# Layer 1's value projections as one of 512 columns with a new order around the first head pairs, and layer 0's stick-breaking weights by sigmoids

## The chip, the core and the metric

The kernel runs as one program on one core of a Trainium2 chip. The core has a matrix engine (TensorE, PE in the profile; its weight loads are PEld), three engines for elementwise work (VectorE or DVE, ScalarE or ACT, GpSimd or POOL), a queue engine that issues most transfers (SyncE, SP), a scratch memory (SBUF) and eight accumulator banks of 128 x 512 fp32 (PSUM) that TensorE writes and the others read. Each engine works through its own list of instructions in order; semaphores between the lists make one engine wait for another. The metric is the device time of one execution in microseconds (us), as the median of several runs.

## The reference, cut to what matters

A decoder trunk with two layers: 256 tokens, width 1024, 16 heads of 64, everything in fp32. Layer 0 mixes by stick-breaking attention, layer 1 by a sparse attention whose keys and values come from one projection of the stream after layer 0; each layer ends with an MLP of 4096 hidden columns and a squared ReLU.

```python
# layer 0, stick-breaking: causal is key < query
z = einsum('bqhd,bshd->bhqs', q, k) * 64 ** -0.5
log_1m = where(causal, log_sigmoid(-z), 0)
excl = cumsum(log_1m, axis=3, reverse=True) - log_1m
a = where(causal, exp(log_sigmoid(z) + excl), 0)
o = einsum('bhqs,bshd->bqhd', a, v)
```

So the weight of a key is sigmoid(z) of that key times the product of sigmoid(-z) over the keys between it and the query.

```python
# layer 1: three branches with gates, keys and values shared by 4 heads
kv = (rms_norm(h) @ w_kv)            # 3 branches x (k, v) x 4 groups x 64
hid = gelu(blk @ cmp_w1); k_cmp, v_cmp = hid @ cmp_w2   # 15 overlapping blocks of 32 tokens
p_cmp = softmax(q . k_cmp / 8)       # compressed branch
p_sel = softmax(rope(q) . k_sel / 8) # selected blocks: 16 of 4, so all of them, causal
p_win = softmax(rope(q) . k_win / 8) # window of 512 tokens, so all of them, causal
out = sum over branches of gate * (p @ v)
```

With 256 tokens both the selected and the window branch are plain causal attention, each with its own keys and values: in each head there are two score matrices, two softmaxes and two products with values, beside the small compressed branch.

## The kernel before, in words

**Precision.** A product of fp32 quality is made of fp32r matmuls: each operand is split into a high part (a cast) and a low part (operand less high part), and `mm3` issues three products, high by high, high by low and low by high. Weights arrive by DMA as `raw` (128x1024), ScalarE casts them to `wh` (L372), VectorE subtracts to get `wl` (L387). All matmuls are issued in L487, all transposes through TensorE in L499.

**What sets the order.** TensorE's list is written out by hand, call by call, in `layer0`, `mlp` and `layer1`. The other engines' lists are made by a planner, `Order`, which runs while the kernel is built: it keeps a clock that each matmul moves on by its estimated cost, and queues of ready steps. A chain (`go(gen, rank)`) is a series of steps, each with an estimated cost and with the engines that may do it: A is ScalarE, D VectorE, G GpSimd. Whenever an engine is free by the planner's clock, it is given the ready step of the lowest rank. `o.need(chain)` ahead of matmuls moves the clock on to the chain's end. The result is a fixed list for each engine; on the chip the engines then run these lists with semaphores, whatever the estimates were.

**Banks.** `B(i, name)` takes PSUM bank i. Matmuls that begin a new tile in a bank wait until the tile that was there has been read out. In layer 1's attention four banks, `Z = (4,5,6,3)`, hold the scores of one head pair; bank 7 holds the accumulator of the q projection (`qp`), banks 1, 2, 0 and sometimes 7 serve the rest.

**Layer 0's attention.** Eight head pairs, two a group. `proj` makes q and k transposed (58 to 64 matmuls between two groups' scores); q is scaled by 0.125 times the token's inverse norm, k by the inverse norm (`rbq`). `scores` writes each head's scores, 384 columns (keys of both blocks for the later queries, of one for the earlier), into a bank. `soft` works on a pair: VectorE takes the minimum with a table (`cap`, 40 where allowed, -1e30 where not) out of PSUM into `sbe`, ScalarE takes exp and ln(1 + x), VectorE runs a scan of sums from the last key to the first that stops at marks (`go_on`), subtracts, and ScalarE takes exp once more (L957 to L965). `turn` transposes the weights, `values` multiplies them with v.

**Layer 1's attention.** `kv_proj` twice (512 columns each: compressed keys and values, then the keys of the other two branches), with the gather of the compressed blocks (`gather_tr`) inside the second; `q_proj` for four groups of four heads, each 48 matmuls of 256 columns in bank 7; `cw_proj` for the compressed blocks' hidden layer. Then eight head pairs, each with

- `scores(p)`: two matmuls of 512 and two of 256 columns into `Z`;
- per pair eight mask passes on VectorE (L1359: add the causal table, minimum as side result), eight exponentials on ScalarE with the sums (L1361), then reciprocal, product with the gates and three scalings of `pe` by L1388 (GpSimd) or L1389 (VectorE);
- `turn(p, 0..2, bank)`: four transposes each into a bank (`ptp`), which ScalarE or VectorE copies to `pT` (L1414).

The value projection is done in two parts, `v_proj(br, 1, ...)`, one a branch, 256 columns for each of the two token blocks, both in bank 1; VectorE or ScalarE evicts each block with its inverse norm (L1119, `vs`). Between these stand the steps of the compressed branch: `cmp_turn` (transposes of the hidden layer, copied to `hidT`, L1466), `cmp_keys`, `cmp_scores` (`psc`), `cmp_soft` (transposes to `psct`, then six small VectorE steps, L1528 to L1537, and two exponentials), `cmp_probs`. `values(g)` multiplies with `vs` and makes the split output `oT` (L576, L577), `part` is a piece of the output projection (`acc`).

The order of the calls in layer 1, cut to the part in question:

```python
v_proj(1, 1, 0, 4); cmp_soft(0, ...)
turn(2, 0, 2); turn(2, 1, 7); v_proj(1, 1, 4, NK)
turn(2, 2, 2); scores(4, Z)
q_proj(3, 7, 0, 4); cmp_probs(0, ...); turn(3, 0, 2); turn(3, 1, 1)
q_proj(3, 7, 4, NK); turn(3, 2, 2)
oc[0] = values(0, 0); cmp_scores(1, 7); scores(5, Z); turn(4, 0, 2)
part(0, 0); ...
```

Of the kernel before, what the change touches and what calls it, by code (L numbers as in the profile page):

```python
# [17 lines left out]
T = 2  # L18
# [10 lines left out]
R_GELU, R_SCT, R_SOFT = 0.7, 0.85, 0.9  # L29
# [5 lines left out]
C_CAP, C_ANY, C_COS, C_SIN, C_BLK, C_PW, C_ROT, C_ROS, C_CMT, C_CB, C_END = (  # L35
    0, 384, 386, 418, 450, 458, 462, 718, 974, 1230, 1486)

SEG = P + 1
ROW = 3 * SEG
# [134 lines left out]
def hybrid_kernel(ctx, tc, x, xt, eye, gcols, gfin, wqk, wv, wo0, wkv, wvs, wq, wg, wo1, w1, w2, cw1, cw2, cpos, gate_b, consts, out):  # L174
# [13 lines left out]
    nc.scalar.preload_act_table_set("natural_log_exp_and_others")  # L188
# [74 lines left out]
    i_kv = [[feed2(wkv[n, i]) for i in range(2)] for n in range(2)]  # L263
    i_c = [[[], []], [[], []]]
    i_vs, i_q = [], []
# [6 lines left out]
    i_q.append(feed2(wq[0]))  # L272
# [544 lines left out]
    def layer0(ap):  # L817
# [84 lines left out]
        rbq = ap.tile([P, 2, T * P], F32, name="rbq", bufs=1)  # L902
# [4 lines left out]
        def rb(i):  # L907
            if i:
                yield dve(256, lambda: nc.vector.tensor_copy(rbq[:, 1, :], pr[:, 0:T * P]))
            else:  # L910
                yield dve(256, lambda: nc.vector.tensor_scalar(rbq[:, 0, :], pr[:, 0:T * P], 0.125, None, op0=OP.mult))

        rbc = [go(rb(i)) for i in range(2)]
# [9 lines left out]
        def proj(p, s0, s1):  # L923
            for s in range(s0, s1):
# [11 lines left out]
                if s % 16 == 15:  # L936
# [3 lines left out]
                    def gen(a=a, qk=qk, q=qkT[:, a]):  # L940
                        u = ap.tile([P, T * P], F32, name="qku", bufs=2)
                        yield act(256, lambda: nc.scalar.copy(u, qk[:, T * P:]))
                        yield dve(256, lambda: nc.vector.tensor_add(q, qk[:, 0:T * P], u))
                        yield rbc[a]
                        yield {"D": (420, lambda: nc.vector.tensor_mul(q, q, rbq[:, a]), True),
                               "G": (620, lambda: nc.gpsimd.tensor_mul(q, q, rbq[:, a]), True)}
                    ch.append(go(gen(), 0.8))

        cap = cst[:, C_CAP:C_CAP + 3 * P].rearrange("p (b c) -> p b c", b=3)

        def soft(z, got):
            e = ap.tile([P, 2 * ROW], F32, name="sbe", bufs=3)
            s = ap.tile([P, 2 * ROW], F32, name="sbs", bufs=2)
            nc.gpsimd.memset(e.rearrange("p (b c) -> p b c", b=6)[:, :, P:SEG], NEG)

            def low(hd):
                return dve(384, lambda: nc.vector.tensor_tensor(  # L957
                    e[:, hd * ROW:(hd + 1) * ROW].rearrange("p (b c) -> p b c", b=3)[:, :, 0:P],
                    z[hd][:, 0:384].rearrange("p (b c) -> p b c", b=3), cap, op=OP.min))
            yield [low(0), low(1)]  # L960
            yield act(774, lambda: nc.scalar.activation(s, e, AF.Exp))
            yield act(774, lambda: nc.scalar.activation(s, s, AF.Ln, bias=1.0))
            yield dve(774, lambda: nc.vector.tensor_tensor_scan(s[:, ::-1], s[:, ::-1], go_on[:, ::-1], 0.0, OP.add, OP.mult), 810, True)
            yield {"D": (956, lambda: nc.vector.tensor_sub(e, e, s), True)}
            yield act(774, lambda: nc.scalar.activation(e, e, AF.Exp))  # L965
            got.append(e)

        def scores(g):
# [7 lines left out]
            for j in range(2):  # L976
# [7 lines left out]
                live["e", 2 * g + j] = got, go(soft(zs[j], got), 1 + 0.01 * g)  # L984
            o.tick(90)

        def turn(g, i, b):
# [5 lines left out]
            for c in range(4):  # L993
# [3 lines left out]
                p0 = hd * ROW + (2, 0, 1)[m] * SEG  # L997
# [78 lines left out]
    def layer1(xk, pt0, ch, ap):  # L1076
# [24 lines left out]
        smallc = go(small(), 3, 6000)  # L1101
# [32 lines left out]
        def value_out(br, t, pk):  # L1134
            yield scaled(vs[t][:, br, :], pk[:, t * 256:(t + 1) * 256], t, 256)
# [4 lines left out]
        def kv_proj(n, banks, mid=None):  # L1140
            pk = [B(b, "pk") for b in banks]
            for k in range(NK):
                if k == 4 and mid is not None:
                    mid()
                if n == 0 and k == 2:
# [22 lines left out]
        def v_proj(br, b, k0, k1):  # L1168
            if k0 == 0:
                pvs[br] = B(b, "pk")  # L1170
            pk = pvs[br]
            for k in range(k0, k1):
                w, c = W(i_vs[br][k // 4]), k % 4 * 256
                for t in range(T):
                    mm3(pk[:, t * 256:(t + 1) * 256], tok(xk, k, t), cut(w, c, c + 256),
                        k == 0 and t == 0, k == NK - 1)
                if k % 4 == 3:
                    gone(i_vs[br][k // 4])
            if k1 < NK:
# [687 lines left out]
```

## Time and profile before

| | |
|---|---|
| median of three runs | 596.75 us (596.1, 596.9, 596.75) |
| the profiled execution | 595.99 us, span 594.2 us |
| value projection and layer 0's attention | about 0 to 27 and 27 to 113 us of the span |
| first MLP | about 113 to 283 us |
| layer 1: projections and attention | about 283 to 418 us, PE busy 134.55 of 135 |
| second MLP and end | about 418 to 594 us |

The rows are of one profiled execution. The page gives for each engine the busy time, its share of the span and the number of instructions; PEclk is the clock that TensorE was granted, in tenths. The chain of waits follows the work that ended last back to the start. In a row of the timeline the columns are start, length, engine, line, operation, what is written and read with its size, and count; in brackets the idle time ahead and what ended it. Rows of groups give busy time, mean length in ns, and the idle time ahead of them. Rows of stretches give the length, then the busy time of PE, PEld, VectorE, ScalarE and GpSimd with counts, the granted clock, the share of the DMA engines and GB/s. The length of a TensorE row holds its drain: matmuls that follow each other overlap, and the distance of two starts is what one costs.

### The profile page before, as it was taken

The numbers are of one execution on the slowest core, as the hardware profiler recorded it, in microseconds if no ns is written. First come the engines' busy times: TensorE is split into PE (matmuls) and PEld (weight loads), VectorE is DVE, ScalarE is ACT, GpSimd is POOL, SyncE is SP. The second block draws the span as 40 slices with busy tenths as digits, with TensorE's granted clock in tenths as the row PEclk, the third lists the DMA queues.
The fourth block names the chain that finished last, engine by engine and source line by source line (L and its number), as shares of the span: only waits on it lengthen the run. The fifth ranks groups of instructions, "written<-read, shape, count | busy, mean of one in ns | idle before, by whom it ended". The sixth has DMA issues, their size and how long they took to land.

```text
span 594.2 us, 9360 instructions
## 1 busy us (share of the span) xinstructions
PE 586.0 (99%) x3346; PEld 492.2 (83%) x3346; DVE 520.0 (88%) x829; ACT 434.9 (73%) x701; POOL 98.3 (17%) x116
## 2 busy tenths in 40 slices
PE   9999999999999999999999999999999999999995
PEld 6888887888888888888888888677888888888884
DVE  6698997589999999998885899964889999999976
ACT  6767667587888978984934796572888888888963
POOL 0013330001211212000120443330001121211001
PEclk9999999999999999999999999999999999999998
DMA  8983334389977899555554634304499787997401
GB/s 317 400 298 105 124 123 148 108 316 372 261 229 235 238 261 265 151 150 185 193 169 152 249 107 156 129 1 141 138 405 322 210 256 217 294 237 225 106 1 71
DMA packets 38063, 119.83 MB, mean 202 GB/s; under 512 B 4608, under 2 KB 5888, under 8 KB 38016
## 3 DMA queue, kind: packets, MB, share of 16 engines
q1 hardware_dynamic: 31248, 107.01, 50.8%
q0 software_dynamic: 6336, 11.54, 11.8%
q10 hardware_dynamic: 432, 0.69, 0.3%
q8 instruction: 26, 0.43, 0.3%
q14 instruction: 21, 0.17, 0.1%
HBM read 118.17 MB, written 1.05 MB: 201 GB/s over the span
## 4 chain that ended last, share of the span: by engine, by line
PE 93%; ACT 4%; DMA 2%; DVE 0%; SPq 0%; issue 0%; POOLq 0%; POOL 0%; ACTq 0%
PE acc L487 34%; PE pu L487 30%; PE qk L487 8%; PE pk L487 4%; PE po L487 3%; PE qp L487 3%; PE pv L487 3%; PE z L487 2%; ACT pe L1361 2%; PE ptp L499 1%; ACT wh L372 1%; DMA rv<-in_wv 1%; PE ph L487 1%; PE pt L499 1%; PE pa L499 1%; DMA raw<-in_wq 1%
## 5 line engine op out<-in xcount | busy, mean ns | idle before, releaser
L387 DVE TENSOR_TENSOR wl<-raw,wh 128x1024 fp32r<-128x1024 f32 x132 | 163.5, 1255 | 11.1 <-ACT wh L372 10.9
L372 ACT CAST wh<-raw 128x1024 fp32r<-128x1024 f32 x132 | 135.6, 1052 | 27.7 <-DMA raw<-in_wq 8.9
L487 PE MATMUL pu<-xn,wh 128*128 128x512 f32 x512 | 128.4, 390 | 0.0
L487 PEld LDWEIGHTS pu<-xn,wh 128*128 128x128 f32 x512 | 94.8, 188 | 18.8
L487 PEld LDWEIGHTS pu<-xn,wl 128*128 128x128 f32 x512 | 70.9, 190 | 5.7
L487 PE MATMUL pu<-xn,wl 128*128 128x256 f32 x512 | 72.6, 282 | 0.0
L487 PE MATMUL acc<-wh,hh 128*128 128x512 f32 (+1 forms) x136 | 53.2, 392 | 0.0
L487 PE MATMUL acc<-wl,hh 128*128 128x512 f32 (+1 forms) x136 | 53.1, 390 | 0.0
L487 PE MATMUL acc<-wh,hl 128*128 128x512 f32 (+1 forms) x136 | 52.7, 388 | 0.0
L674 ACT COPY mu<-pu 128x512 f32<-128x512 f32 x64 | 37.4, 584 | 19.1 <-PE pu L487 18.9
L394 POOL DMA_DIRECT2D fours<-in_w x24 | 21.5, 896 | 147.5 <-DVE ms L707 69.4
L487 PE MATMUL acc<-wh,oT 128*128 128x512 f32 x128 | 43.2, 401 | 0.0
L394 POOL DMA_DIRECT2D four<-in_w x20 | 19.5, 977 | 142.2 <-DMA four<-in_w 65.0
L696 DVE TENSOR_TENSOR hl<-ms,hh 128x1024 fp32r<-128x1024 f32 (+2 forms) x36 | 36.4, 1014 | 3.3 <-ACT hh L695 2.9
L487 PE MATMUL acc<-th,hh 128*128 128x512 f32 x96 | 37.7, 393 | 0.0
L487 PE MATMUL acc<-tl,hh 128*128 128x512 f32 x96 | 37.6, 392 | 0.0
L487 PE MATMUL acc<-th,hl 128*128 128x512 f32 x96 | 37.4, 389 | 0.0
L695 ACT CAST hh<-ms 128x1024 fp32r<-128x1024 f32 (+2 forms) x36 | 31.6, 884 | 2.6 <-DVE ms L707 2.3
L487 PE MATMUL pk<-wh,xk 128*128 128x512 f32 (+1 forms) x128 | 32.9, 340 | 0.0
L1361 ACT ACTIVATE pe<-pe,nm 128x256 f32<-128x256 f32 (+1 forms) x64 | 28.5, 448 | 5.6 <-DVE nm L1359 5.6
L487 PE MATMUL qk<-xa,wh 128*128 128x512 f32 x128 | 32.5, 395 | 0.0
L1388 POOL TENSOR_TENSOR pe<-pe,rs 128x512 f32<-128x512 f32 x17 | 22.1, 1315 | 50.0 <-DVE rs L1378 42.8
(225 smaller groups left out, 1224.2 us busy)
## 6 DMA issues: line engine op xcount, KB each, us to landing
raw<-in_w SPq DMA_DIRECT2D x80, 512.0 KB, 6.2
four<-in_w SPq DMA_DIRECT2D x24, 512.0 KB, 6.9
fours<-in_w SPq DMA_DIRECT2D x24, 512.0 KB, 7.6
raw<-in_wqk SPq DMA_DIRECT2D x16, 512.0 KB, 6.1
raw<-in_wo SPq DMA_DIRECT2D x16, 512.0 KB, 4.0
fours<-in_w POOLq DMA_DIRECT2D x24, 256.0 KB, 4.9
four<-in_w POOLq DMA_DIRECT2D x20, 256.0 KB, 6.6
raw<-in_wkv SPq DMA_DIRECT2D x8, 512.0 KB, 4.5
```

Of the source, the lines that this page charges most:

```text
L372: k = {"A": (195 + 0.835 * m, lambda: nc.scalar.copy(a, b), False), "D": (200 + 0.49 * m, lambda: nc.vector.tensor_copy(a, b), True)}
L387: yield {"D": (150 + 1.045 * m, lambda: nc.vector.tensor_sub(lo, raw, f32(hi)), True)}
L394: nc.gpsimd.dma_start(to, other, accum_op=OP.add)
L487: nc.tensor.matmul(o_, a, b, start=first, stop=last, skip_group_check=True)
L499: nc.tensor.transpose(o_, a, i)
L674: yield act(512, lambda: nc.scalar.copy(u[:, f, :], pu[f]))
L695: yield act((b - a) * P, lambda: nc.scalar.copy(hh[:, into], flat[:, q]))
L696: yield dve((b - a) * P, lambda: nc.vector.tensor_sub(hl[:, into], flat[:, q], f32(hh[:, into])), port=True)
L1361: act(n, lambda: nc.scalar.activation(d, d, AF.Exp, bias=nm[:, i:i + 1], scale=-1.0, accum_out=rs[:, t, hd, b:b + 1]), 150)]
L1388: return {"G": (1040, lambda: nc.gpsimd.tensor_tensor(s, s, f, op=OP.mult), True), "D": (690, lambda: nc.vector.tensor_tensor(s, s, f, op= ...
```

## The change

**Layer 1's values.** One projection of 512 columns (both branches) takes the place of two of 256. It has an accumulator for each token block, in banks 1 and 7, and its weights are stored and fetched in blocks of 512 columns. VectorE or ScalarE evicts 512 columns at once.

**Layer 1's list of calls** is rewritten: the scores and transposes of the first pairs come earlier, the value projection stands in four pieces between pairs 1 and 4, the steps of the compressed branch stand elsewhere, and the transposes of pairs 0 to 3 use other banks. The weights are fetched in the new order of use, on the same queue. The second `kv_proj` is called in two pieces with the gather between. The planner's ranks of the copies of q's input (2.5 to 1.0) and of the small tables (3 to 1.5) change, `scores` lets the planner wait until the former pair's scores were read (`zread`), and slots of `pT` and of the gathered blocks change places.

**Layer 0's weights.** Scores are no longer scaled by q's inverse norm; a sigmoid reads them out of PSUM with the token's scale, 0.125 times the inverse norm, with a minus for the factors of the product and a plus for the key's own weight: eight sigmoids a pair, four of 256 and four of 128 columns. VectorE's scan multiplies, with a 1 added at each query's own place (`begins`, an identity written by ScalarE), so that masked keys come out as zero; one product follows. The minimum with `cap`, the exponentials and the logarithm of the weights are gone. The table of functions that ScalarE loads at the start is the one with the sigmoid; the one with exp and ln is loaded in layer 1.

```diff
@@ feeds
-    i_q.append(feed2(wq[1]))
-    feed_cw(1)
-    i_vs.append(feed2(wvs[0]))
-    i_q.append(feed2(wq[2]))
-    i_vs.append(feed2(wvs[1]))
-    i_q.append(feed2(wq[3]))
+    feed_q(1)
+    feed_cw(1)
+    feed_q(2)
+    feed_v()
+    feed_q(3)
...
@@ layer0
-            yield [low(0), low(1)]
-            yield act(774, lambda: nc.scalar.activation(s, e, AF.Exp))
-            yield act(774, lambda: nc.scalar.activation(s, s, AF.Ln, bias=1.0))
-            yield dve(774, lambda: nc.vector.tensor_tensor_scan(s[:, ::-1], s[:, ::-1], go_on[:, ::-1], 0.0, OP.add, OP.mult), 810, True)
-            yield {"D": (956, lambda: nc.vector.tensor_sub(e, e, s), True)}
-            yield act(774, lambda: nc.scalar.activation(e, e, AF.Exp))
+            def sig(to, hd, t, i):
+                src = z[hd][:, 0:256] if t else z[hd][:, 256:384]
+                dst = to[:, hd * HW:hd * HW + 256] if t else to[:, hd * HW + 257:hd * HW + 385]
+                return act(128 + 128 * t, lambda: nc.scalar.activation(dst, src, AF.Sigmoid, scale=by[:, t, i:i + 1]), 95)
+            yield begun
+            yield byc
+            yield [sig(f, hd, t, 0) for t in (1, 0) for hd in range(2)]
+            nc.gpsimd.memset(e.rearrange("p (h c) -> p h c", h=2)[:, :, 256:HW:129], 0.0)
+            yield [dve(772, lambda: nc.vector.tensor_tensor_scan(
+                f[:, ::-1], f[:, ::-1], begins[:, ::-1], 0.0, OP.mult, OP.add), 810, True)] + [
+                sig(e, hd, t, 1) for t in (1, 0) for hd in range(2)]
+            yield {"D": (956, lambda: nc.vector.tensor_mul(e[:, 0:2 * HW - 1], e[:, 0:2 * HW - 1], f[:, 1:2 * HW]), True)}
...
@@ layer1
-        def value_out(br, t, pk):
-            yield scaled(vs[t][:, br, :], pk[:, t * 256:(t + 1) * 256], t, 256)
+        def value_out(t):
+            yield scaled(vs[t].rearrange("p b c -> p (b c)"), pvs[t], t, 512)
...
+        def v_proj(k0, k1):
+            for t in range(T if k0 == 0 else 0):
+                pvs[t] = B((1, 7)[t], "pk")
             for k in range(k0, k1):
-                w, c = W(i_vs[br][k // 4]), k % 4 * 256
+                w, c = W(i_vs[k // 2]), k % 2 * 512
                 for t in range(T):
-                    mm3(pk[:, t * 256:(t + 1) * 256], tok(xk, k, t), cut(w, c, c + 256),
-                        k == 0 and t == 0, k == NK - 1)
+                    mm3(pvs[t], tok(xk, k, t), cut(w, c, c + 512), k == 0, k == NK - 1)
...
+            if k1 == NK:
+                vsc.extend(go(value_out(t), 1.1) for t in range(T))
...
+        q_proj(1, 7, 0, 2)
         scores(0, Z)
-        q_proj(1, 7)
+        q_proj(1, 7, 2, 6)
+        scores(1, Z)
+        q_proj(1, 7, 6, NK)
         cw_proj(1)
         hc = go(gelu(), R_GELU)
-        scores(1, Z)
-        v_proj(0, 1, 0, 4)
         turn(0, 0, 2)
-        turn(0, 1, 0)
-        v_proj(0, 1, 4, NK)
+        turn(0, 1, 1)
         turn(0, 2, 2)
         q_proj(2, 7, 0, 2)
-        cmp["tc"] = cmp_turn(0)
         scores(2, Z)
-        q_proj(2, 7, 2, 4)
+        q_proj(2, 7, 2, 5)
+        turn(1, 0, 2)
+        turn(1, 1, 0)
+        q_proj(2, 7, 5, NK)
+        cmp["tc"] = cmp_turn(1)
+        turn(1, 2, 2)
+        v_proj(0, 2)
         cmp["kc"] = cmp_keys(0)
-        q_proj(2, 7, 4, 5)
-        turn(1, 0, 2)
-        turn(1, 1, 1)
-        q_proj(2, 7, 5, NK)
-        turn(1, 2, 2)
+        scores(3, Z)
+        v_proj(2, 4)
         cmp["s0"] = cmp_scores(0, 0)
-        scores(3, Z)
-        v_proj(1, 1, 0, 4)
-        cmp["s0"] = cmp_soft(0, *cmp["s0"], 0)
         turn(2, 0, 2)
-        turn(2, 1, 7)
-        v_proj(1, 1, 4, NK)
+        turn(2, 1, 2)
+        v_proj(4, 6)
         turn(2, 2, 2)
         scores(4, Z)
+        cmp["s0"] = cmp_soft(0, *cmp["s0"], 0)
+        v_proj(6, NK)
         q_proj(3, 7, 0, 4)
+        turn(3, 0, 2)
+        turn(3, 1, 2)
+        q_proj(3, 7, 4, 6)
+        scores(5, Z)
         pcc[0].append(cmp_probs(0, cmp["s0"], 0))
-        turn(3, 0, 2)
-        turn(3, 1, 1)
-        q_proj(3, 7, 4, NK)
+        q_proj(3, 7, 6, NK)
         turn(3, 2, 2)
         oT = o_tiles(0)
         oc[0] = values(0, 0)
+        turn(4, 0, 2)
         cmp["s1"] = cmp_scores(1, 7)
-        scores(5, Z)
-        turn(4, 0, 2)
         part(0, 0)
```

The lists that the planner made of it, at three places. A name with a number is one buffer of that name; a bracket names the engines whose semaphores the instruction waits for.

TensorE's list before, from the end of the second value projection (`pk`) over the last transposes of pair 2 (`ptp`) and the scores of pair 4 (`z`) to the first matmuls of q of group 3 (`qp`, bank 7):

```order
L487 MATMUL pk<-wl,xk 128x256
L487 MATMUL pk<-wh,xk 128x256
L499 MATMUL ptp<-ident,pe 128x128 [waits Activation_49]
L499 MATMUL ptp<-ident,pe 128x128 x3
L487 MATMUL z_3817<-kT,qm 128x512
L487 MATMUL z_3818<-kT,qm 128x512
L487 MATMUL z_3819<-kT,qm 128x256
L487 MATMUL z_3820<-kT,qm 128x256
L487 MATMUL qp<-xq,wh 128x256 [waits Activation_49]
```

and now:

```order
L497 MATMUL psct<-cw2s,hv 120x64 x4
L509 MATMUL psct<-ident,sct 128x128 x2
L497 MATMUL pk<-wh,xk 128x512
L497 MATMUL pk<-wl,xk 128x512
L497 MATMUL pk<-wh,xk 128x512 x2
...
L497 MATMUL pk<-wh,xk 128x512
L497 MATMUL qp<-xq,wh 128x256 [waits DVE_49]
L497 MATMUL qp<-xq,wh 128x256
L497 MATMUL qp<-xq,wl 128x256
```

The scores and transposes that stood between the last value matmul and q of group 3 now stand ahead of the last 12 value matmuls; q's first matmul follows these directly and waits for VectorE.

VectorE's list now, from the copy of pair 2's second transposes to the evictions of the two value accumulators (`vs`); mask passes of pair 4 (L1383), steps of the compressed softmax (`cmx`, `ce`, `csm`), a weight split (`wl`) and a scaling of pair 3 (L1415):

```order
L1440 COPY pT<-ptp 128x512
L1404 TENSOR_TENSOR rs<-rs,gates 128x8
L397 TENSOR_TENSOR wl<-raw,wh 128x1024
L1383 ISA pe,nm<-z_3741,causal 128x256
...
L1554 TENSOR_REDUCE cmx<-psct 128x16
...
L1415 TENSOR_TENSOR pe<-pe,rs 128x512
...
L1562 TENSOR_TENSOR csm<-csm,gany 128x16
...
L1563 TENSOR_TENSOR ce<-ce,csm 128x240
L1383 ISA pe,nm<-z_3744,causal 128x128
L1383 ISA nm 128x1
L1139 TENSOR_SCALAR vs_2919<-pk,r 128x512
L1139 TENSOR_SCALAR vs_2920<-pk,r 128x512
```

Before, the evictions of 256 columns stood ahead of the mask passes of pair 4; now they stand behind all eight (four of 256 columns and four of 128) and behind the softmax.

TensorE's list at the first two transposes of pair 2, before:

```order
L487 MATMUL psct<-cw2s,hv 120x64 x3
L499 MATMUL psct<-ident,sct 128x128 x2
L499 MATMUL ptp<-ident,pe 128x128 [waits DVE_49,Activation_49]
L499 MATMUL ptp<-ident,pe 128x128 [waits Pool_49]
L499 MATMUL ptp<-ident,pe 128x128
L499 MATMUL ptp<-ident,pe 128x128 [waits Activation_49]
L499 MATMUL ptp<-ident,pe 128x128 x3
L499 MATMUL ptp<-ident,pe 128x128 [waits Pool_49]
L487 MATMUL pk<-wh,xk 128x256
```

and now (`psc` are the compressed scores):

```order
L497 MATMUL psc<-qu,kcb 32x256 [waits DVE_49,PE_49]
L497 MATMUL psc<-qu,kcb 32x256 x3
L509 MATMUL ptp<-ident,pe 128x128 [waits DVE_49,Activation_49]
L509 MATMUL ptp<-ident,pe 128x128 [waits Pool_49]
L509 MATMUL ptp<-ident,pe 128x128
L509 MATMUL ptp<-ident,pe 128x128 [waits Activation_49]
L509 MATMUL ptp<-ident,pe 128x128 [waits DVE_49]
L509 MATMUL ptp<-ident,pe 128x128 x2
L509 MATMUL ptp<-ident,pe 128x128 [waits Pool_49]
L497 MATMUL pk<-wh,xk 128x512
```

The second four transposes, which went to bank 7, now go to bank 2 as the first four do, and their first one waits for VectorE, which copies the first four.

More of the change, by code (lines that the diff above doesn't have):

```diff
@@ L33 @@
 GELU_C = 2.0 * 0.7978845608028654
[L35 to L39, printed above, removed]
+C_ANY, C_COS, C_SIN, C_BLK, C_PW, C_ROT, C_ROS, C_CMT, C_CB, C_END = (
+    0, 2, 34, 66, 74, 78, 334, 590, 846, 1102)
+HW = 3 * P + 2
 LAG = 200
@@ L262, in hybrid_kernel, with feed_kv, feed_q, feed_v @@
     i_m = [feed_mlp(0)]
-    i_kv = [[feed2(wkv[n, i]) for i in range(2)] for n in range(2)]
+    i_kv = [None, None]
     i_c = [[[], []], [[], []]]
-    i_vs, i_q = [], []
+    i_vs, i_q = [], [None] * NG
+    def feed_kv(n):
+        i_kv[n] = [feed2(wkv[n, i]) for i in range(2)]
+    def feed_q(g):
+        i_q[g] = feed2(wq[g])
+    def feed_v():
+        for i in range(2):
+            i_vs.extend(feed2(wvs[i]))
     def feed_cw(i):
@@ L893, in layer0, with starts @@
         pump()
-        go_on = ap.tile([P, 2 * ROW], BF16, name="go_on", bufs=1)
-        nc.gpsimd.memset(go_on, 1.0)
-        nc.gpsimd.memset(go_on.rearrange("p (h c) -> p h c", h=2)[:, :, 2 * SEG - 1:ROW:SEG], 0.0)
+        begins = ap.tile([P, 2 * HW], BF16, name="begins", bufs=1)
+        nc.gpsimd.memset(begins, 0.0)
+        fs = [ap.tile([P, 2 * HW], F32, name=f"sbf{i}", bufs=1) for i in range(2)]
+        for f in fs:
+            nc.gpsimd.memset(f, 0.0)
+        def starts():
+            b2 = begins.rearrange("p (h c) -> p h c", h=2)
+            for c in (P, 2 * P + 1):
+                yield act(256, lambda: nc.scalar.copy(b2[:, :, c:c + P], ident[:, None, :].to_broadcast([P, 2, P])))
+        begun = Chain(o, starts(), 1.5, ws.landed)
         v_first(0)
@@ L905, in layer0, with rb, scale @@
             mm(pr[:, t * P:(t + 1) * P], rstd[t].to_broadcast([P, P]), ident, t == 0, True, 4.0)
[L907 to L913, printed above, removed]
+        def rb():
+            yield dve(256, lambda: nc.vector.tensor_copy(rbq, pr[:, 0:T * P]))
+        def scale():
+            for t in range(T):
+                for i in range(2):
+                    yield dve(1, lambda: nc.vector.tensor_scalar(by[:, t, i:i + 1], rstd[t], (-0.125, 0.125)[i], None, op0=OP.mult))
+        rbc, byc = go(rb()), go(scale())
         def v_out(n, t):
@@ L1132, in key_out, with kv_proj @@
             yield pool(128, lambda: nc.gpsimd.tensor_add(src[:, :, 0:16], a, b), 60)
-        def value_out(br, t, pk):
-            yield scaled(vs[t][:, br, :], pk[:, t * 256:(t + 1) * 256], t, 256)
+        def value_out(t):
+            yield scaled(vs[t].rearrange("p b c -> p (b c)"), pvs[t], t, 512)
         def first_out(t, pk):
             yield scaled(kd0[:, t], pk.rearrange("p (m d) -> p m d", d=DH), t, 512)
[L1140 to L1144, printed above, removed]
+        pks = {}
+        def kv_proj(n, banks, k0, k1):
+            if k0 == 0:
+                pks[n] = [B(b, "pk") for b in banks]
+            pk = pks[n]
+            for k in range(k0, k1):
                 if n == 0 and k == 2:
@@ L1337, in scores @@
             o.need(qch[g], *kc)
+            o.need(*zread)
+            zread.clear()
             z1 = [B(banks[hd], "z1").rearrange("p (b k) -> p b k", b=2) for hd in range(2)]
@@ L1541, in cmp_probs @@
         def cmp_probs(f, c, b):
-            o.need(c)
+            o.need(c, *pcc[f])
             pt = B(b, "pct")
```

85 lines of the change are left out of this document (40 added, 45 removed).

## The prediction

> **What bounds the kernel now.** Read the page's busy times first, then the chain that ended last, then stretches of 10 us.
>
> ```profile
> span 594.2 us, 9360 instructions
> PE 586.0 (99%) x3346; PEld 492.2 (83%) x3346; DVE 520.0 (88%) x829; ACT 434.9 (73%) x701; POOL 98.3 (17%) x116
> PEclk9999999999999999999999999999999999999998
> PE 93%; ACT 4%; DMA 2%; DVE 0%; SPq 0%; issue 0%; POOLq 0%; POOL 0%; ACTq 0%
> ```
>
> TensorE is busy for 99% of the span, at a clock that is granted throughout, and 93% of the last chain is its own matmuls. So the end moves only with what TensorE issues and with the time in which it stands still. The other engines count only where they make it wait. How near that is differs by stage:
>
> ```profile
> 60.00:70.00 10.00, 10.00 (x62) 8.92 (x61) 10.00 (x11) 7.59 (x12) 4.30 (x3) 1.00 0.18 59
> 340.00:350.00 10.00, 10.00 (x81) 8.21 (x82) 9.72 (x28) 10.00 (x23) 3.18 (x3) 1.00 0.35 124
> 350.00:360.00 10.00, 9.58 (x79) 8.54 (x78) 9.92 (x33) 8.47 (x29) 6.23 (x5) 1.00 0.21 70
> 360.00:370.00 10.00, 10.00 (x86) 8.74 (x86) 9.79 (x30) 7.84 (x23) 3.01 (x4) 1.00 0.53 179
> ```
>
> The columns are the stretch, its length, then busy time of PE, PEld, DVE, ACT and POOL. In layer 1's attention (the last three rows) VectorE is as full as TensorE: what is queued late there comes late, and TensorE notices as soon as nothing stands between it and the result. Layer 0's attention (the first row) is as full, but there TensorE has long projections to do meanwhile.
>
> **What is taken off TensorE.** The value projections and the one wait of that stage:
>
> ```profile
> 301.53 5.49 PE pk L487 x24
> 356.50 2.87 PE pk L487 x24
> 353.77 0.95 PE L487 MATMUL psct<-cw2s,hv 128*120 128x64 f32 x8
> 354.56 0.39 PE L499 MATMUL psct<-ident,sct 128*128 128x128 f32 x2
> 355.37 1.14 PE L499 MATMUL ptp<-ident,pe 128*128 128x128 f32 x8 [0.42 <-ACT pe L1361]
> 364.59 0.87 PE ptp L499 x8
> ```
>
> 24 matmuls of 512 columns take 5.49 us, 228.8 ns each; 24 of 256 take 2.87, 119.6 each. Before, 96 of 256: 11.48 us. Now 48 of 512: 10.98. **-0.5.** (The Trainium skill, "TensorE: Matmul & The Clock Gate", section Back-to-back issue gap, gives N/2.4 + 2.5 ns from one lone matmul to the next; by it a pair of 256 would lose only 2.5 ns, the part would be -0.1 and the sum 0.4 higher. The rows give four times that, and I go by them.) A transpose is 0.87/8 = 0.109 us, so after 354.56 TensorE was free at 354.78 and began at 355.37: a wait of 0.6, which the new order, with the transposes of pair 2 elsewhere, need not have. **-0.6.**
>
> **What is added: banks that are written again at once.** A PSUM bank that is to be written anew must first have been read out. The new list puts both value accumulators in banks 1 and 7, so that the transposes beside them have bank 2 alone, and it moves the scores that used to stand between. The price of a turnaround:
>
> ```profile
> 348.21 0.60 PE L499 MATMUL ptp<-ident,pe 128*128 128x128 f32 x4
> 345.17 1.03 PE L499 MATMUL ptp<-ident,pe 128*128 128x128 f32 x8
> 346.24 0.59 ACT L1414 COPY pT<-ptp 128x512 f32<-128x512 f32 x1
> 354.04 1.19 DVE L1389 TENSOR_TENSOR pe<-pe,rs 128x512 f32<-128x512 f32 x1
> L1414 ACT COPY pT<-ptp 128x512 f32<-128x512 f32 x16 | 9.2, 579 | 6.5 <-PE ptp L499 6.5
> L1414 DVE COPY pT<-ptp 128x512 f32<-128x512 f32 x8 | 5.5, 690 | 2.4 <-PE ptp L499 2.2
> ```
>
> Four transposes issue in 0.44 and end after 0.60: 0.16 of drain. The copy begins 0.04 later (346.20 to 346.24) and takes 0.58 on ScalarE or 0.69 on VectorE; TensorE restarts 0.14 after its releaser (354.04 + 1.19 = 355.23, then 355.37; the row of the transposes names ScalarE, but this scaling ended last). Sum 0.92 to 1.03.
>
> - Pair 0: its three turns follow each other in banks 2, 1, 2. 0.92 less the 0.44 of the turn between: **+0.5**. Before, half a value projection stood there.
> - Pair 2: two turns in bank 2 with nothing between, and a mask pass (0.35) ahead of VectorE's copy: **+1.2**. Pair 3 the same, with nothing ahead: **+1.0**.
> - The hidden layer's transposes go to bank 1, then four transposes (0.44), then the value projection takes bank 1. On ScalarE the copy of q stands ahead of the hidden layer's copy, and waits for the last q matmul:
>
> ```profile
> L1466 ACT COPY hidT<-pht 128x240 f32<-128x240 f32 x1 | 0.4, 360 | 0.0
> 371.79 0.60 PE L487 MATMUL po<-pcT,vcb 120*64 120x256 f32 x4
> 372.44 0.59 ACT L576 CAST oT<-po 128x512 fp32r<-128x512 f32 x1 [2.61 <-PE po L487]
> 373.06 0.69 DVE L577 TENSOR_TENSOR oT<-po,oT 128x512 fp32r<-128x512 f32 x1
> 372.89 1.56 PE L487 MATMUL z<-kT,qm 64*128 64x512 f32 x8
> 374.80 0.48 PE L487 MATMUL acc<-wh,oT 128*128 128x512 f32 x1
> ```
>
>   0.16 + 0.04 + 0.48 (a following copy starts 0.1 before the end) + 0.36 + 0.14 = 1.18, less six transposes, 0.65: **+0.5**.
> - The first output projection needs the values' two splits, done at 373.06 + 0.69 = 373.75, and came at 374.80. The scores between (1.49 of issue) are gone from there, so it would come at 373.31: 0.44 + 0.14, and 0.2 for a wait in ScalarE's or VectorE's queue: **+0.8**.
>
> **The large one: q of group 3 in bank 7.** It starts directly behind the last value matmul, and its first matmul writes the bank in which the second value accumulator still lies; in the built program it waits for VectorE. Before, values lay in bank 1 and q alone in 7. What VectorE has queued ahead of that eviction is in the order above: the copy, the small product and the weight split, then eight mask passes of pair 4, the compressed softmax, half a scaling of pair 3, two evictions.
>
> ```profile
> 352.16 0.41 DVE L1359 CUSTOM_DVE_ANT_0 pe<-z,causal 128x256 f32<-128x256 f32 x1
> 352.50 0.28 DVE L1359 CUSTOM_DVE_ANT_0 pe<-z,causal 128x128 f32<-128x128 f32 x1
> 352.71 0.28 DVE L1359 CUSTOM_DVE_ANT_0 pe<-z,causal 128x128 f32<-128x128 f32 x1
> L1389 DVE TENSOR_TENSOR pe<-pe,rs 128x512 f32<-128x512 f32 x7 | 7.0, 997 | 0.1
> L1528 DVE TENSOR_REDUCE cmx<-psct 128x16 f32<-128x240 f32 x2 | 0.8, 400 | 0.0
> L1536 DVE TENSOR_TENSOR csm<-csm,gany 128x16 f32<-128x16 f32 x2 | 1.1, 565 | 0.0
> L387 DVE TENSOR_TENSOR wl<-raw,wh 128x1024 fp32r<-128x1024 f32 x22 | 29.2, 1332 | 0.4 <-ACT wh L372 0.4
> ```
>
> Masks start 0.34 and 0.21 apart: eight are 2.2. The scaling 1.0. Six small steps of the softmax (maximum, difference, sum, reciprocal, product, scaling) I take at 0.35, between the maximum's 0.40 and what 16 columns should need (the product's 0.57 is a mean of two), less the 0.07 by which a mask starts before the last one ends: 1.7. Two evictions of 512 columns by the copy's row, 0.62 and 0.69: 1.3. Together 6.2. They start late: copy, product and split (0.2 + 0.62 + 0.12 + 1.2, from where the scores of pair 4 begin, which take 1.49) put the first mask 0.65 after the scores. So bank 7 is free 6.2 + 0.65 + 0.2 = 7.05 after the scores. TensorE has till then the 1.0 from 353.77 to 354.78 and 12 matmuls, 2.74: 3.75. **+3.3.**
>
> Bounds: at least one eviction with its turnaround, 1.0, if VectorE were otherwise empty; 4.6 if a second weight split (1.33) stands in that queue. I take the sum, as it is a queue in order on an engine that is 98% busy there. For the turnarounds the bounds are the bare ones (0.5, 0.9, 0.9, 0.1, 0.4) and a weight split more (1.3) at any of them.
>
> **What is moved and costs nothing.** Layer 0's weights. Rows of the old form and the nearest one to a sigmoid out of PSUM with a scale per partition:
>
> ```profile
> L961 ACT ACTIVATE sbs<-sbe 128x774 f32<-128x774 f32 x8 | 6.8, 849 | 9.3 <-DVE sbe L957 9.3
> L957 DVE TENSOR_TENSOR sbe<-z,cst 128x384 f32<-128x384 f32 x16 | 7.8, 545 | 0.0
> L964 DVE TENSOR_TENSOR sbe<-sbe,sbs 128x774 f32<-128x774 f32 x8 | 8.8, 1111 | 0.1
> L548 ACT ACTIVATE xn<-pt,gc 128x256 fp32r<-128x256 f32 x4 | 1.6, 476 | 5.1 <-PE pt L499 5.1
> 58.56 10.65 PE qk L487 x58
> 313.99 0.59 ACT L1318 COPY qu<-qp 128x512 f32<-128x512 f32 x1 [4.90 <-DVE qm L1319]
> L188 ACT ACT_TABLE_LOAD x1 | 1.3, 1283 | 0.7 <-PEq L1857 0.7
> ```
>
> Per pair ScalarE loses three passes (2.55) and gets eight sigmoids, about 4 x 0.48 + 4 x 0.37 = 3.4; VectorE loses two passes (1.1). For a group of two pairs: 16 sigmoids start about 0.1 closer than they last, 5.2 us; then the last product, 1.1: some 7 with a cast between. TensorE does 58 projection matmuls, 10.65, before it wants them. If that cover were gone, the excess would be paid once a group, four times. The second table load (1.28) falls into ScalarE's 4.90 of idle time ahead of q's copy. The stick-breaking relief of VectorE in layer 0 gains nothing, as TensorE doesn't wait there. The scores of pairs 0 and 1 that come earlier have 24 matmuls (2.9) between them against eight masks (2.2); the order of the weights' loads only follows that of their use.
>
> **Sum:** -0.5 - 0.6 + 0.5 + 1.2 + 1.0 + 0.5 + 0.8 + 3.3 = +6.2. The profiled execution took 595.99 (span 594.2 and 1.8 around it), 0.76 under the median 596.75 of the three; 602.2 against the one, 602.95 against the other. I say 602.5.
>
> **Rivals.**
> - *The evictions come in time* (faster). For it: TensorE's 99% and the small waits seen so far. Against it: the turns behind each other leave nothing to overlap with. Only the 1.1 of savings would stay: 594.9 against the one execution, 595.65 against the median, 595.3 between. It decides if all six waits together stay under 1.1. 8%. The Trainium skill, "PSUM — Partial Sum Buffer", section PSUM bank collisions raise a hardware error, wants PSUM guarded by semaphores by bank, since the chip itself doesn't stall; no run here shows a collision, but by it no write may slip under a read.
> - *VectorE is less late at bank 7.* The softmax steps and the split take their shortest, and the masks start with the scores: 2.0 instead of 3.3, and the bare turnarounds, 2.8 in all: 595.99 + 2.8 + 2.0 - 1.1 = 599.7, or 600.0 by the same middle. 15%.
> - *Layer 0 becomes late.* If a sigmoid takes 0.15 more than its neighbour, 16 of them add 2.4 a group, and the first group, whose begin marks must be written too, overruns by a microsecond, to 603.5, and with a second group late as well to 604. 8%.
> - *The added waits cancel with waits that I overlook in the old order* (no change). The three stretches show 0.4 of idle PE in 30 us, so there is little to cancel: 596.75. 5%.
>
> The likeliest, 602.5, has 64%. Range 598.8 to 605: the lower end takes in VectorE's lesser lateness, the upper one the bound of 4.6 and one more split (1.3) at a turnaround. A measurement of this kernel tells about 0.2% (1.2 us) from no change. Slower 0.87 (64 + 15 + 8), same 0.05, faster 0.08.
>
> **What will show it.** In the profile after: PE idle of 2 to 5 us ahead of a qp matmul released by a VectorE eviction vs<-pk of 512 columns; two waits of about 1 us ahead of ptp released by pT copies; pk matmuls at 228 ns; no PE idle ahead of pa in layer 0; the same MLP stretches. A dense PE row through that stage, or a wait in layer 0, would prove me wrong.

## The result, and the profile after

The changed kernel takes 604.54 us (median of four executions, 603.51 to 605.17), the kernel before beside it 596.45 (596.1 to 596.9): a ratio of 1.0134, with a 95% interval of 1.0122 to 1.0146. It is slower by 8.1 us. The profiled execution took 603.51, with a span of 601.7 against 594.2.

Its page, the busy times and the chain:

```profile
PE 587.9 (98%) x3298; PEld 490.6 (82%) x3298; DVE 513.4 (85%) x821; ACT 437.1 (73%) x739; POOL 84.9 (14%) x107
PE 96%; DVE 2%; ACT 0%; issue 0%; POOLq 0%; POOL 0%; ACTq 0%
```

VectorE has 6.6 us less to do than before, and TensorE is still what ends last: the time went into TensorE standing still. Where, the same stretches show (length, then busy time of PE, PEld, DVE, ACT, POOL):

```profile
60.00:70.00 10.00, 10.00 (x61) 8.83 (x60) 9.40 (x11) 6.24 (x14) 1.44 (x2) 1.00 0.34 112
350.00:360.00 10.00, 9.09 (x55) 6.31 (x54) 8.79 (x27) 6.33 (x20) 3.82 (x3) 1.00 0.46 150
360.00:370.00 10.00, 6.95 (x46) 5.85 (x45) 6.08 (x27) 6.22 (x20) 1.74 (x2) 1.00 0.18 62
```

Layer 0 is as dense as before; in layer 1, 10 us from 360 on hold 6.95 of PE. The view of waits, for TensorE alone (who waits, for whom, us in total, times, longest), first before, then after:

```profile
...
PE ptp L499 <- ACT pe L1361: 0.4, 1, 0.4
...
```

```profile
PE qp L497 <- DVE vs L1139: 2.7, 1, 2.7
PE ptp L509 <- DVE pT L1440: 1.7, 2, 0.9
PE acc L497 <- DVE oT L587: 0.9, 1, 0.9
...
PE ptp L509 <- ACT pT L1440: 0.3, 1, 0.3
PE pk L497 <- ACT hidT L1492: 0.3, 1, 0.3
```

The one wait of 0.4 in front of transposes is gone, and six others are there. The timeline of the changed kernel gives them one by one:

```profile
332.87 1.09 PE L509 MATMUL ptp<-ident,pe 128*128 128x128 f32 x8
334.25 0.66 PE L509 MATMUL ptp<-ident,pe 128*128 128x128 f32 x4 [0.29 <-ACT pT L1440]
...
343.25 0.60 PE L509 MATMUL ptp<-ident,pe 128*128 128x128 f32 x4
344.14 0.50 PE L497 MATMUL pk<-wh,xk 128*128 128x512 f32 x1 [0.28 <-ACT hidT L1492]
...
352.48 0.65 PE L509 MATMUL ptp<-ident,pe 128*128 128x128 f32 x4
354.04 0.66 PE L509 MATMUL ptp<-ident,pe 128*128 128x128 f32 x4 [0.91 <-DVE pT L1440]
...
362.98 0.39 PE L497 MATMUL pk<-wh,xk 128*128 128x512 f32 x1
366.03 0.50 PE L497 MATMUL qp<-xq,wh 128*128 128x256 f32 x2 [2.67 <-DVE vs L1139]
...
369.01 0.60 PE L509 MATMUL ptp<-ident,pe 128*128 128x128 f32 x4
370.39 0.66 PE L509 MATMUL ptp<-ident,pe 128*128 128x128 f32 x4 [0.78 <-DVE pT L1440]
...
380.33 0.64 PE L497 MATMUL psc<-qu,kcb 128*32 128x256 f32 x8
381.88 0.50 PE L497 MATMUL acc<-wh,oT 128*128 128x512 f32 x1 [0.92 <-DVE oT L587]
```

The bracket counts from the modelled end of the last matmul, so it leaves out the drain that a wait uncovers. What a wait costs is the distance of the two starts less what the earlier instructions issue in: 334.25 - 332.87 - 8 x 0.109 = 0.51; 344.14 - 343.25 - 0.44 = 0.45; 354.04 - 352.48 - 0.44 = 1.12; 366.03 - 362.98 - 0.23 = 2.82; 370.39 - 369.01 - 0.44 = 0.94; 381.88 - 380.33 - 0.56 = 0.99 (0.56 is what the same eight took before, with the scores behind them). Together 6.83.

The stage as a whole, from the first matmul of the compressed blocks to the first transpose of the second MLP, before and after:

```profile
315.86 0.65 PE L487 MATMUL ph<-raw,blk 128*64 128x256 f32 x4
...
414.75 0.27 PE L499 MATMUL pt<-ident,hres 128*128 128x128 f32 x1
```

```profile
316.10 0.65 PE L497 MATMUL ph<-raw,blk 128*64 128x256 f32 x4
...
421.82 0.27 PE L509 MATMUL pt<-ident,hres 128*128 128x128 f32 x1
```

98.89 before, 105.72 after: +6.83 here, of the span's +7.5; 0.24 came before this stage, the rest behind the last matmul. In the stage 6.83 were added by the six waits, 0.58 saved with the old wait, and 0.35 with the values (the distances from each value matmul to the next start add up to 11.85 before and 11.50 after, the long wait left out). That leaves 0.9, in many small distances.

VectorE's timeline ahead of the large wait, with the passes between left out:

```profile
359.76 0.42 DVE L1383 CUSTOM_DVE_ANT_0 pe<-z,causal 128x256 f32<-128x256 f32 x1
...
360.64 0.41 DVE L1554 TENSOR_REDUCE cmx<-psct 128x16 f32<-128x240 f32 x1 [0.46 <-PE psct L509]
...
361.83 0.69 DVE L1415 TENSOR_TENSOR pe<-pe,rs 128x512 f32<-128x512 f32 x1
...
364.57 1.41 DVE L1139 TENSOR_SCALAR vs<-pk,r 128x512 f32<-128x512 f32 x2
```

From the first mask at 359.76 to the evictions at 364.57 there are 4.81 of masks, softmax and scaling with one gap of 0.46 (for the compressed scores), then 1.41 of evictions; TensorE has been out of other work since 363.2.

### The profile page after: what moved, and what is told of

Same layout as the page of the kernel before. It is cut to its first block, busy times and chain, and to the rows that moved or that the text cites. A ratio compares the mean times of both kernels' runs of the same rounds, so it can differ in the third digit from the quotient of the medians.

```text
span 601.7 us, 9287 instructions
## 1 busy us (share of the span) xinstructions
PE 587.9 (98%) x3298; PEld 490.6 (82%) x3298; DVE 513.4 (85%) x821; ACT 437.1 (73%) x739; POOL 84.9 (14%) x107
## 3 DMA queue, kind: packets, MB, share of 16 engines
HBM read 117.97 MB, written 1.05 MB: 198 GB/s over the span
## 4 chain that ended last, share of the span: by engine, by line
PE 96%; DVE 2%; ACT 0%; issue 0%; POOLq 0%; POOL 0%; ACTq 0%
PE acc L497 34%; PE pu L497 30%; PE qk L497 8%; PE pk L497 5%; PE qp L497 4%; PE pv L497 4%; PE z L497 3%; PE po L497 3%; PE ptp L509 2%; PE ph L497 1%; PE pt L509 1%; PE pa L509 1%; PE warm L497 1%; DVE pe L1383 0%; DVE wl L397 0%; PE gp L497 0%
## 5 line engine op out<-in xcount | busy, mean ns | idle before, releaser
L497 PE MATMUL pk<-wh,xk 128*128 128x512 f32 x96 | 31.4, 396 | 0.3 <-ACT hidT L1492 0.3
L497 PEld LDWEIGHTS acc<-wh,hl 128*128 128x128 f32 x136 | 25.5, 188 | 5.5
```

The lines of the kernel that those rows point to most:

```text
L497: nc.tensor.matmul(o_, a, b, start=first, stop=last, skip_group_check=True)
```

## The experiments

Each was compared with the kernel before, run beside it: 596.59 for the first four, 596.07 for the next three, 596.06 (one execution) for the last four.

### Layer 0 alone, layer 1 alone

The first is the kernel before with all of the change's edits in layer 0, and with the second table of functions loaded behind the second `kv_proj`:

```diff
-    nc.scalar.preload_act_table_set("natural_log_exp_and_others")
+    nc.scalar.preload_act_table_set("sigmoid_and_others")
...
-            yield act(774, lambda: nc.scalar.activation(s, e, AF.Exp))
...
+            yield [sig(f, hd, t, 0) for t in (1, 0) for hd in range(2)]
...
         kv_proj(1, (2, 3), gathers)
...
+        go(tables(), 1)
```

> The kernel before with the sigmoids of layer 0 alone. Theory (all of the loss is TensorE standing still in layer 1): no wait of TensorE is added in layer 0, since the projections there still cover ScalarE and VectorE; 596.4 plus or minus 0.6, where the 0.6 is the later start seen in the profile (first scores 41.67 against 41.34) and the spread of the runs. Rival (layer 0 carries what the six named waits leave over, 8.1 less 5.7): 597.5 to 599.

597.01, ratio 1.0006 (0.9997 to 1.0015): no difference that can be told from the spread. The median lies at the forecast's upper end (597.0) and under the rival's 597.5. No wait of TensorE is added in layer 0; beside the one at the start, the view has only the old wait of layer 1:

```profile
...
PE ptp L498 <- ACT pe L1370: 0.5, 1, 0.5
```

The second is the changed kernel with those edits taken back:

```diff
-    nc.scalar.preload_act_table_set("sigmoid_and_others")
+    nc.scalar.preload_act_table_set("natural_log_exp_and_others")
...
-            yield [sig(f, hd, t, 0) for t in (1, 0) for hd in range(2)]
...
+            yield act(774, lambda: nc.scalar.activation(s, e, AF.Exp))
...
-        go(tables(), 1)
```

> The changed kernel with the old weights of layer 0. Theory: all of the loss is in layer 1, so 603.5 to 604.8, and the same six waits (0.46, 0.45, 1.07, 2.83, 0.95, 1.0) ahead of the same instructions. Rival (layer 0 carries two of the eight microseconds): 602 to 602.6.

604.44, ratio 1.0122 (1.0105 to 1.0139), with the six waits at the same places. So layer 1's part alone makes the loss, and the rival is out. But the profile had something that the changed kernel's first profile did not. Behind the large wait:

```profile
365.54 0.61 PE L498 MATMUL qp<-xq,wh 128*128 128x256 f32 x2 [2.66 <-DVE vs L1130]
365.95 0.41 PE L498 MATMUL qp<-xq,wl 128*128 128x256 f32 x1
366.16 0.63 PE L498 MATMUL qp<-xq,wh 128*128 128x256 f32 x2
```

The starts lie 0.21 apart here (365.54 for two, then 365.95 and 366.16), not 0.12, and the stretch behind the wait was granted half the clock:

```profile
363.00:366.00 3.00, 0.46 (x3) 0.46 (x4) 2.48 (x11) 3.00 (x11) 0.00 (x0) 0.96 0.00 0
366.00:369.00 3.00, 3.00 (x16) 3.00 (x16) 0.20 (x1) 0.15 (x2) 0.00 (x0) 0.50 0.00 0
```

### Other work between the last value matmul and q

```diff
         turn(2, 2, 2)
+        v_proj(6, NK)
         scores(4, Z)
         cmp["s0"] = cmp_soft(0, *cmp["s0"], 0)
-        v_proj(6, NK)
         q_proj(3, 7, 0, 4)
```

> The changed kernel with one line moved: the last quarter of the value projection stands ahead of the scores of pair 4, so that scores and the small products of the compressed branch lie between the last value matmul and q of group 3, and the evictions are ready before the mask passes of pair 4 are. Theory (bank 7 waits for an eviction that is queued behind those masks): the wait of 2.83 ahead of q falls under 0.3; the first output projection comes earlier, and its wait may grow by up to 1; 1.8 to 2.8 under the changed kernel, 601.7 to 602.7. Rival (VectorE is behind by that much whatever stands first in its list, and whoever needs it next waits): the wait comes back ahead of the transposes of pair 3 and the output projection; 603.8 to 604.5.

601.25, ratio 1.0072 (1.0057 to 1.0087).

```profile
PE ptp L509 <- DVE pT L1440: 1.7, 2, 0.9
PE acc L497 <- DVE oT L587: 1.5, 1, 1.5
...
```

The wait ahead of q is gone, that of the output projection grew by 0.6, as far as the theory allowed, and the others stayed. The rival wanted all of the 2.8 to come back, so it is out. The span fell from 601.7 to 599.4, by 2.3: 2.8 less 0.6. The median fell by 3.3, by 1.0 more than the forecast's middle and 0.5 below its lower end; that fits the clock, which has no long wait to fall behind now: the profile shows it full, and the mean clocks listed for the four executions are 0.996 to 0.998.

### Transposes apart

```diff
+        v_proj(4, 5)
         turn(2, 1, 2)
-        v_proj(4, 6)
+        v_proj(5, 6)
...
-        turn(3, 1, 2)
         q_proj(3, 7, 4, 6)
+        turn(3, 1, 2)
```

> The changed kernel with the second transposes of pair 2 six value matmuls later and those of pair 3 twelve q matmuls later, so that work of 1.4 us lies between two transposes into bank 2. Theory (the price is the turnaround of one bank): the waits of 1.07 and 0.95 fall to 0.2 or less each, the wait ahead of q stays at 2.8; 602.6 to 603.2. Rival (TensorE just comes earlier to the same VectorE): the wait ahead of q grows by what is saved ahead of it, 1.07; 603.6 or more.

602.08, ratio 1.0089 (1.0072 to 1.0106); the executions took 601.38, 601.39, 602.77 and 603.25.

```profile
PE qp L497 <- DVE vs L1139: 2.7, 1, 2.7
PE acc L497 <- DVE oT L587: 1.2, 1, 1.2
PE warm L497 <- PEq L1886: 0.8, 1, 0.8
...
```

The view is sorted by time, and both waits on pT's copies by VectorE are gone from it. The wait ahead of q has not grown: VectorE's queue moved forward together with TensorE's (its first mask still starts 0.44 behind the scores of pair 4, the evictions 4.81 behind that mask). The rival is out. The median lies 0.5 under the forecast's lower end. Its four times lie in two groups 1.4 to 1.9 apart, which fits a clock that falls behind the wait of 2.7 in some executions: the mean clock listed is 0.997 for the two short ones and 0.994 for the two long ones.

### The evictions earlier in the planner's list

```diff
-                vsc.extend(go(value_out(t), 1.1) for t in range(T))
+                vsc.extend(go(value_out(t), 0.5) for t in range(T))
```

> The changed kernel with the planner's rank of the two value evictions at 0.5 instead of 1.1, so that they stand ahead of most mask passes of pair 4 in VectorE's (or ScalarE's) list; TensorE's list is as in the changed kernel. Theory (the wait ahead of q is the queue in front of the evictions): the wait falls from 2.83 to 0.9 to 1.6, no wait of TensorE reaches 2.5 us, so its clock stays full; 601.4 to 602.8. Rival (the masks that now come later are missed instead, at the scores of pair 5 or the transposes): 603.3 to 604.5.

602.85, ratio 1.0112 (1.0097 to 1.0128), with executions from 602.57 to 602.93. The upper end of the forecast was 602.8: the wait fell less than expected, to 1.8 by the bracket and 1.9 by the starts, not to 1.6 or less.

```profile
363.19 0.39 PE L497 MATMUL pk<-wh,xk 128*128 128x512 f32 x1
365.35 0.50 PE L497 MATMUL qp<-xq,wh 128*128 128x256 f32 x2 [1.77 <-ACT vs L1138]
```

The releaser is ScalarE now. The planner gave it the eviction of bank 7, and there it stands behind a weight cast (ScalarE's timeline):

```profile
363.66 1.04 ACT L382 CAST wh<-raw 128x1024 fp32r<-128x1024 f32 x1 [0.47 <-ACT pe L1385]
364.61 0.68 ACT L1138 ACTIVATE vs<-pk,r 128x512 f32<-128x512 f32 x1
```

A better rank only chooses among the steps that are ready when the planner gives an engine its next one; here the cast stands ahead of the eviction in ScalarE's list. The masks that moved back were not missed anywhere (the other waits grew by 0.2 at most, and one fell by 0.1), so the rival's mechanism did not show. The clock stayed full in the profile, and the four times lie within 0.4.

### The eviction doubled

```diff
-            yield scaled(vs[t].rearrange("p b c -> p (b c)"), pvs[t], t, 512)
+            def twice():
+                for _ in range(2):
+                    nc.vector.tensor_scalar(vs[t].rearrange("p b c -> p (b c)"), pvs[t], rstd[t], None, op0=OP.mult)
+            yield dve(512, twice, 65)
```

> The changed kernel in which VectorE evicts each of the two value accumulators twice, with the same result; all lists keep their order. Theory in two steps: the wait ahead of q grows by two passes of 0.6 to 0.7, from 2.83 to about 4.2; and a wait of this length lets TensorE's clock fall, as in the profile with layer 1's part alone (0.55 granted over 3.8 us behind the wait, q's matmuls at 0.215 instead of 0.120 us), now in every run: 1.4 + 1.6 over a run in which it does not fall (603.5), so 606 to 607, with a clock of about 0.5 behind the wait. Rival (the fall of the clock was a chance of that one run): 604.5 + 1.4, so 605.9 at most, and a clock of 1.0 behind the wait. Rival (the eviction is not what q waits for): 604.5.

606.17, ratio 1.0171 (1.0158 to 1.0185). The wait was 4.2, and behind it:

```profile
PE qp L497 <- DVE vs L1157: 4.2, 1, 4.2
...
364.80:368.21 3.41, 0.60 (x5) 0.60 (x6) 2.79 (x5) 1.85 (x10) 0.00 (x0) 1.00 0.00 0
368.21:371.63 3.42, 3.42 (x19) 3.42 (x18) 0.00 (x0) 0.00 (x0) 0.00 (x0) 0.50 0.00 0
```

q does wait for this eviction, and the clock fell. The median lies in the theory's range, but only 0.3 over the 605.9 of the rival, with executions from 605.76 to 607.05; the clock decides it. The same kernel, executed and profiled once more:

> The kernel with the doubled evictions once more (wait of 4.2 us ahead of q). Theory: a wait this long always costs the clock, so 0.5 to 0.6 for 3 to 4 us behind it again. Rival: 1.0 this time.

605.83, and again a lowered clock:

```profile
366.00:369.00 3.00, 1.95 (x9) 1.96 (x10) 1.07 (x3) 0.08 (x1) 0.00 (x0) 0.58 0.00 0
```

### Three further executions of the changed kernel

> The changed kernel as it is, another profiled execution. In its first profile the wait of 2.7 us ahead of q left the clock at 1.0; in the kernel with layer 1's part alone the same wait let it fall to 0.55. Theory (the fall follows a wait of this length in some executions, at random): of three further executions of the changed kernel at least one shows 0.5 to 0.6 behind the wait and takes about 1.5 us longer than one that doesn't. Rival (the fall belongs to the other kernel, or to the chip): all three at 1.0.

> The second of the three further executions of the changed kernel, with the same two answers to tell apart as for the first.

> The third of the three further executions of the changed kernel, with the same two answers to tell apart as for the first.

604.51, 604.06 and 605.09. The stretch from 366 to 369 in the first, second and third:

```profile
366.00:369.00 3.00, 3.00 (x16) 3.00 (x16) 0.20 (x1) 0.00 (x0) 0.00 (x0) 0.52 0.00 0
```

```profile
366.00:369.00 3.00, 2.50 (x21) 2.50 (x22) 0.65 (x2) 1.12 (x6) 0.00 (x0) 1.00 0.00 0
```

```profile
366.00:369.00 3.00, 2.85 (x13) 2.85 (x14) 0.30 (x2) 0.76 (x4) 0.00 (x0) 0.50 0.00 0
```

With the first profile that is two executions with a full clock, 603.51 and 604.06, and two with a fallen one, 604.51 and 605.09. The means differ by 1.0. In the traces q's first 24 matmuls take 1.49 and 1.36 more where the clock fell (1.49 with layer 1's part alone, 1.47 and 1.22 with the eviction doubled): 16 and 14 of the distances between their starts are 0.2 or more, in the two others only the first. So the fall follows the wait in some executions only, and the rival is out.

Which ones, the traces' record of the granted clock shows. In all five profiles with a fall in layer 1 the low stretch is 3.41 us long, and the full stretches between two changes last 228.69, 232.11, 361.81, 587.09 or 590.51 us, which is 67, 68, 106, 172 and 173 times 3.413. So the clock changes only at the marks of a grid of 3.41 us, and the grid lies differently against the kernel in each execution. Cut at these marks, the first profile of the changed kernel and the first further one:

```profile
361.57:364.98 3.41, 1.80 (x8) 1.13 (x6) 3.41 (x19) 2.94 (x10) 0.17 (x1) 1.00 0.33 120
364.98:368.40 3.42, 2.37 (x19) 2.37 (x20) 1.20 (x3) 1.66 (x8) 0.00 (x0) 1.00 0.00 0
```

```profile
362.08:365.49 3.41, 0.75 (x4) 0.30 (x3) 3.24 (x14) 2.94 (x11) 0.00 (x0) 1.00 0.03 12
365.49:368.90 3.41, 3.41 (x17) 3.41 (x18) 0.20 (x1) 0.50 (x4) 0.00 (x0) 0.50 0.00 0
```

In the first a mark cuts the same wait in two, 1.61 and 1.05 of idle TensorE; in the other all 2.66 lie between two marks, and the clock falls at the second. Over all profiles it fell after each such piece with 1.78 or more of idle time (at the waits ahead of q 2.36 to 3.41; the 1.78 is at the last matmuls of the third further execution) and after none with 1.73 or less (that one with the transposes apart). So about half an idle piece is what it takes here.

### All waits repaired

```diff
-        turn(0, 2, 2)
         q_proj(2, 7, 0, 2)
+        turn(0, 2, 2)
...
-        cmp["tc"] = cmp_turn(1)
+        cmp["tc"] = cmp_turn(0)
...
+        v_proj(4, 5)
         turn(2, 1, 2)
-        v_proj(4, 6)
+        v_proj(5, 6)
         turn(2, 2, 2)
+        v_proj(6, NK)
         scores(4, Z)
...
-        v_proj(6, NK)
...
-        turn(3, 1, 2)
         q_proj(3, 7, 4, 6)
+        turn(3, 1, 2)
...
+        turn(4, 1, 3)
         part(0, 0)
         cmp["s1"] = cmp_soft(1, *cmp["s1"], 7)
-        turn(4, 1, 2)
         part(0, 1)
```

> The changed kernel with the waits taken away where a place for other work was found: last quarter of the values ahead of the scores of pair 4; second transposes of pairs 2 and 3 apart from the first; two q pieces between the second and third transposes of pair 0; the hidden layer's transposes in bank 0; the second transposes of pair 4 (bank 3) ahead of the first output projection. Theory (the loss is these waits, and each ends when work stands in between): of the waits 0.3 to 0.7 each are left at two or three places, the gain of 0.4 from 512 columns and of 0.6 from the old wait stays, and about 0.6 for more changes between kinds of matmuls; 596.6 to 598. Rival (VectorE's lateness only moves on): 599.5 or more.

598.38, ratio 1.0044 (1.0031 to 1.0057): 0.4 above the range. Four of the five executions took 598.14 to 598.55; why the fifth took 600.19, nothing here shows.

```profile
...
PE ptp L509 <- POOL pe L1414: 0.6, 1, 0.6
PE acc L497 <- DVE oT L587: 0.6, 1, 0.6
```

It is 2.3 over the kernel before, of 8.1 at first, so the waits, with the clock that falls behind them, are most of the loss. It still doesn't come down to the kernel before: two waits of 0.6 are left, one of them new (the last transpose of pair 1's first two turns now comes before GpSimd has scaled that pair), and the smaller gaps stay. No version that was run beats the kernel before.

## Why the prediction was right

**Direction and place.** All six added waits came where the prediction put them, ahead of the named instructions and with the named releasers, and layer 0 added none: the projections there do cover the sigmoids. The sigmoids took 0.48 and 0.52 for 256 columns and 0.39 and 0.41 for 128, where the prediction took 0.48 from a neighbour's row and 0.37 from none; the old wait went too.

**The sizes** (us, forecast and what the starts give):

| term | forecast | measured |
|---|---|---|
| values at 512 columns | -0.5 | -0.35 |
| old wait | -0.6 | -0.58 |
| pair 0's turns | +0.5 | +0.51 |
| pair 2's turns | +1.2 | +1.12 |
| pair 3's turns | +1.0 | +0.94 |
| hidden layer's copy | +0.5 | +0.45 |
| output projection | +0.8 | +0.99 |
| q in bank 7 | +3.3 | +2.82 |
| **sum** | **+6.2** | **+5.9** |

The turnaround of a bank, added up from drain, copy and restart, held within 0.1 in four places (pairs 0, 2 and 3 and the hidden layer), partly by luck: TensorE restarted 0.05 behind a copy (353.99 to 354.04 for pair 2) and not 0.14, and at pairs 0 and 2 the copy began 0.1 later than the bare sum had it. For pair 2 the prediction's own terms, 1.03 and a mask pass of 0.35, make 1.38 and not the 1.2 that it wrote; the mask was half done when the transposes ended. The output projection cost 0.2 more because its split stood in VectorE's list behind a weight split that took 2.10, while the cast that it needs had ended 0.5 earlier (380.66, and the split began at 381.15).

The large term was 0.5 too high, though the queue itself was 6.22 (4.81 and 1.41) against 6.2. There two errors cancelled: the scaling of pair 3 took 0.69, not the 1.0 of its row's mean, and the gap of 0.46 had no term. The 0.5 lies around the queue: the first mask followed the scores by 0.44, not 0.65; q restarted 0.05 behind the evictions (365.98 to 366.03), not 0.2; and TensorE had 3.89 of other work, not 3.75.

**What was missing.** The forecast was 2.0 low, 602.5 for 604.54, and the sum is not to blame, since its terms came 0.3 lower. Two things had no term. First the clock: the prediction took the price of a wait to end with the wait, but in two of the four profiled executions q's matmuls then ran at half speed for about 3 us, 1.4 to 1.5 on top. (Of the four executions behind the median only the first, at 603.51, was profiled; that the others are longer by the clock is likely, not shown.) Second the 0.9 that the stage holds beside the waits. By the distances between starts it lies where TensorE changes from one kind of matmul to another (q, scores, transposes, values). There are about as many changes as before (60 and 61), but four runs of q matmuls end at scores now, none before; these four distances of 0.21 make 0.84, and all others together change by 0.1. No run isolated it. The remaining few tenths lie ahead of layer 1 and behind the last matmul, within what executions of one kernel differ by.

**The rivals.** "The evictions come in time" and "no change" fell with the six waits; "less late at bank 7" with 2.82 against its 2.0; "layer 0 becomes late" with layer 0 alone at 1.0006.

## What to carry to other kernels

Where TensorE is full and the other engines nearly so, a saving of half a microsecond in matmuls can cost many times that in accumulator banks: ask of every bank which instruction reads it last (on VectorE or ScalarE; in these traces GpSimd reads none), what is queued ahead of that one on its engine, and what TensorE has to do meanwhile. A turnaround of a bank costs 0.9 to 1.1 us here unless other work of that length stands in between, and a line moved (values ahead of scores) was worth more than a better rank for the eviction (3.3 against 1.7 by the medians). A wait of TensorE should be priced together with the clock behind it, 1.2 to 1.5 us here, once it is longer than about 1.7 us: by the 1.73 and 1.78 above, and as an estimate, a wait of 2.7 us costs it in about three of four positions of the grid, one of 3.5 us always.

## What the runs showed of the hardware that was not expected

TensorE's clock fell to half for 3.41 us behind a wait of 2.7 us, in three of six profiles with such a wait (two of four of the changed kernel and the one with layer 1's part alone, not the one with the transposes apart); behind 4.2 us in both profiles taken, behind 1.8 us not in the one taken. It fell at the end of a piece of a 3.41 us grid in which TensorE was idle for 1.78 us or more, so the same wait costs the clock in one execution and not in the next.

The Trainium skill, "TensorE: Matmul & The Clock Gate", section What's actually happening, describes a gate that passes half the pulses after an idle window of about 3.4 us, and says that the window runs freely, so that the same kernel differs from execution to execution. The traces agree with half the clock (0.50), with the window's length (3.41) and with its running freely; but a window needed to be idle for only about half of it (1.78 us was enough, 1.73 was not), where the page speaks of an idle one. Whether half is the exact limit, no run here shows.
